# Where the matmul streams and the weights' low halves start in SBUF: the starting bytes modulo 512 of xs, y, z and `lo`

## The chip, the core and the metric

The kernel runs on one core of a Trainium2 chip. The metric is the device time of one execution in microseconds, taken as the median of several runs. A profile of one further execution is read beside it; its span goes from the first to the last recorded instruction.

## The reference

Two residual blocks over 256 tokens of width 2048, in float32. Block 0 mixes with a gated causal convolution of width 31 on one half of the channels and with windowed means on the other; block 1 mixes with a gated causal convolution of width 3. After each mixer stands a gated feed-forward of width 5632.

```python
def conv_pool_mixer(x, ...):
    u = rms_norm(x, norm_g) @ w_in
    a = a_val * sigmoid(a_gate)
    a = silu(layer_norm(causal_depthwise_conv(a, conv_w) + conv_b, ln_g, ln_b))
    p = multiscale_pool(b_in, w_pool, pool_scale)
    return concatenate([a, p], axis=-1) @ w_out

def short_conv_mixer(x, ...):
    u = rms_norm(x, norm_g) @ w_in
    return (gate_b * causal_depthwise_conv(gate_c * v, conv_w)) @ w_out

def swiglu(h, w_gate, w_up, w_down):
    return (silu(h @ w_gate) * (h @ w_up)) @ w_down

def reference(...):
    h = x
    for i in range(DEPTH):
        mixer = conv_pool_mixer if i % 2 == 0 else short_conv_mixer
        h = h + mixer(h, ...)
        h = h + swiglu(rms_norm(h, ffn_norm[i]), w_gate[i], w_up[i], w_down[i])
    return rms_norm(h, final_norm)
```

## The kernel before

**The arithmetic.** Features lie on the 128 partitions and the 256 tokens along the free dimension. Every matrix product runs in the type float32r, with both operands split in two: a weight block of 128 x 128 becomes a rounded high half `hi` (a cast on ScalarE, line 124) and the remainder `lo` (a subtraction on VectorE, line 131; for some pieces of the first mixer on GpSimd). An activation chunk becomes 256 columns of high half followed by 256 columns of remainder, 512 columns or 2048 bytes per partition in one tile (`xs`, `y`, `z` or `cat`). Three of the four products are kept. In a *wide* product (lines 173 and 174) `hi` meets all 512 columns and then `lo` meets the first 256. In a *narrow* one (lines 176 to 178) there are three steps of 256 columns: `hi` with the first half, `hi` with the second, `lo` with the first.

**The weights.** All weights stand in HBM as one row of blocks in the order of use. `fetch` (line 110) brings them in units of up to 16 blocks by DMAs that SyncE issues; `prepare` (line 116) turns pieces of 8 blocks into one `hi` and one `lo` tile each, up to four pieces ahead of use (six buffers of each); `next_block` (line 134) hands them to `product` (line 171). TensorE loads the weights of a step by an instruction of its own, recorded beside the matmul of the step before.

**The stages.** They run one after the other, each a long chain of products with nothing of TensorE's work between:

- first mixer, narrow, 656 blocks: projection from `xs`, pooling and output products from `cat` and `xs`;
- first feed-forward, wide, in two halves of the hidden width. Each half has 22 hidden chunks with two products of 16 blocks from `xs` (704 pairs) and then 16 output chunks of 22 blocks from `y` (352 pairs): 1056 pairs;
- second mixer, wide: 16 chunks of three products from `xs` (768 pairs), then 16 output chunks of 16 blocks from `z` (256 pairs): 1024 pairs;
- second feed-forward, like the first; the last output chunk from `y` is narrow (22 blocks).

`Norm` (line 286) fills `xs` chunk by chunk behind the output product of the stage before; `swiglu` (line 555) fills `y`; the loop at line 586 fills `z`.

**Where the tiles start.** `moving(room, at, n)` (line 222) gives a view of a tile from byte `at` of each partition on. The constants of lines 78 to 85 are these `at`. Blocks, chunks and buffers are whole multiples of 512 bytes long, so the starting byte modulo 512 is the same for every chunk of a stream and for every block of all `hi` or `lo` buffers. From the program's placement of the tiles:

| tile | first byte of the tile | `at` | start modulo 512 | past `hi` modulo 512 |
|---|---|---|---|---|
| `hi` (six buffers) | 101952 | 0 | 64 | 0 |
| `lo` (six buffers) | 126528 | 0 | 64 | 0 |
| `xs`, first mixer | 36160 | 32 | 352 | 288 |
| `xs`, later stages | 36160 | 160 | 480 | 416 |
| `y`, both feed-forwards | 159392 | 64 | 224 | 160 |
| `z` | 159392 | 64 | 224 | 160 |
| `cat` | 184928 | 0 | 96 | 32 |

Of the kernel before, what the change touches and what calls it, by code (L numbers as in the profile page):

```python
# [12 lines left out]
F32R = mybir.dt.float32r  # L13
# [4 lines left out]
P = 128  # L18
T = 256
D = 2048  # L20
NC = D // P
# [4 lines left out]
NH = NF // 2  # L26
# [38 lines left out]
UNIT_AT = [sum(UNITS[:u]) for u in range(len(UNITS))]  # L65

PIECE = 8
PIECES = [(u, o, min(PIECE, n - o)) for u, n in enumerate(UNITS) for o in range(0, n, PIECE)]

LOOK = 4  # L70
AHEAD = 1

# [3 lines left out]


XS_M0 = 32
XS_F0 = 160
XS_M1 = 160  # L80
XS_F1 = 160
Y_F0 = 64
Y_F1 = 64
Z_M1 = 64
CAT = 0

POOL_SPLIT = range(96, 24 * NC + 16 + 7 * NC + 8)
# [7 lines left out]
def block_kernel(ctx: ExitStack, tc: tile.TileContext, xT: bass.AP, xtok: bass.AP, vec: bass.AP, wall: bass.AP, out: bass.AP):  # L95
    nc = tc.nc
    const = ctx.enter_context(tc.tile_pool(name="const", bufs=1))
    act = ctx.enter_context(tc.tile_pool(name="act", bufs=1))
    wst = ctx.enter_context(tc.tile_pool(name="wst", bufs=4))
    whl = ctx.enter_context(tc.tile_pool(name="whl", bufs=6))  # L100
# [9 lines left out]
    def fetch(u):  # L110
        if u < len(UNITS) and u not in loaded:
            n, off = UNITS[u], UNIT_AT[u] * P * P
            loaded[u] = w = wst.tile([P, 16 * P], F32, name="w")
            nc.sync.dma_start(w[:, : n * P], wall[off : off + n * P * P].rearrange("(p f) -> p f", p=P))  # L114

    def prepare(i):
        if i >= len(PIECES) or i in ready:
            return
        u, o, n = PIECES[i]
        fetch(u)  # L120
        w = loaded[u][:, o * P : (o + n) * P]
        hi = whl.tile([P, PIECE * P], F32R, name="hi")
        lo = whl.tile([P, PIECE * P], F32R, name="lo")
        nc.scalar.copy(hi[:, : n * P], w)  # L124
        engine = nc.vector
        if UNIT_AT[u] + o in POOL_SPLIT:
            if relief:
                relief.pop()
            else:
                engine = nc.gpsimd  # L130
        engine.tensor_tensor(out=lo[:, : n * P], in0=w, in1=hi[:, : n * P], op=ALU.subtract)  # L131
        ready[i] = (hi, lo)

    def next_block():
        b, i = cursor
        at = UNIT_AT[PIECES[i][0]] + PIECES[i][1]
        if b == at + PIECES[i][2]:
            ready.pop(i)
            i, at = i + 1, b
        for j in range(i, i + LOOK + 1):  # L140
            prepare(j)
        if i + LOOK < len(PIECES):
            for u in range(PIECES[i + LOOK][0] + 1, PIECES[i + LOOK][0] + AHEAD + 1):
                fetch(u)
        cursor[:] = [b + 1, i]
        hi, lo = ready[i]
        o = (b - at) * P
        return hi[:, o : o + P], lo[:, o : o + P]
# [16 lines left out]
    def drain():  # L165
        while any(queues.values()):
            for q in queues.values():
                if q:
                    q.popleft()[1]()
# [10 lines left out]
    def matmul_chunks(xs, ks, n=1, wide=False, behind=None):  # L180


        accs = [ps.tile([P, 2 * T], F32, name="acc") for _ in range(n)]
        for i, k in enumerate(ks):
            first, last = i == 0, i == len(ks) - 1
            for acc in accs:
                hi, lo = next_block()
                product(acc, hi, lo, xs[:, k, :], first, last, wide)
                tick()
            if behind is not None:  # L190
                behind(k)
        return accs
# [10 lines left out]
    def split(dst, src, scale=None):  # L203

        if scale is None:
            nc.scalar.copy(dst[:, :T], src)
            nc.vector.tensor_tensor(out=dst[:, T:], in0=src, in1=dst[:, :T], op=ALU.subtract)
        else:
            nc.scalar.activation(dst[:, :T], src, AF.Copy, scale=scale)
            nc.vector.scalar_tensor_tensor(out=dst[:, T:], in0=src, scalar=scale, in1=dst[:, :T], op0=ALU.mult, op1=ALU.subtract)  # L210
# [6 lines left out]

    identity = v[:, VECS["identity"] :]
    h = act.tile([P, NC, T], F32, name="h")
    xs_room = act.tile([P, NC * 2 * T + 64], F32R, name="xs")  # L220

    def moving(room, at, n):

        return room[:, at // 4 : at // 4 + n * 2 * T].rearrange("p (c t) -> p c t", c=n)
# [99 lines left out]
    def project(src, ks, norm=None, wide=False, narrow_end=False):  # L324

        for n in range(NC):
            if narrow_end and n == NC - 1:
                wide = False
            (acc,) = matmul_chunks(src, ks, wide=wide)
            if wide:  # L330
                t = phase[0].tile([P, T], F32, name="cross", bufs=3)
                nc.scalar.copy(t, acc[:, T:])
                nc.vector.tensor_tensor(out=h[:, n, :], in0=h[:, n, :], in1=t, op=ALU.add)
            nc.vector.tensor_tensor(out=h[:, n, :], in0=acc[:, :T], in1=h[:, n, :], op=ALU.add)  # L334
            if norm is not None:
                norm.add(n)

    def scaled(acc, r, name, wide=False):
        if not wide:
            s = (phase[0] if name == "pv" else tmp).tile([P, T], F32, name=name, bufs=2)  # L340
            nc.vector.tensor_tensor(out=s, in0=acc[:, :T], in1=r, op=ALU.mult)
            return s
        s = summed(acc, name)
        nc.vector.tensor_tensor(out=s, in0=s, in1=r, op=ALU.mult)
        return s
# [3 lines left out]
    xs = norm.xs  # L349
# [20 lines left out]
    rowsq = const.tile([P, 2], F32, name="rowsq")  # L370
    load(0, 1)
    prepare(0)
    prepare(1)
    load(1, 1)
    prepare(2)
# [8 lines left out]
    with tc.tile_pool(name="m0", bufs=1) as m0, tc.tile_pool(name="ps_side", bufs=2, space=PSUM) as ps_side:  # L384
# [166 lines left out]
        drain()  # L551
        norm = Norm("ffn_norm0", XS_F0)
        project(cat, range(NA), norm)

    def swiglu(norm, following, at):
        with tc.tile_pool(name="ffn", bufs=1) as fp:
            phase[0] = fp
            y = moving(fp.tile([P, NH * 2 * T + 32], F32R, name="y"), at, NH)
            r = None
            for half in range(2):  # L560
                for f in range(NH):
                    (acc_g,) = matmul_chunks(norm.xs, every, wide=True)
                    (acc_u,) = matmul_chunks(norm.xs, every, wide=True)
                    if r is None:
                        r = norm.rstd()
                    gate = scaled(acc_g, r, "gate", True)
                    up = scaled(acc_u, r, "val", True)
                    nc.scalar.activation(gate, gate, AF.Silu)
                    nc.vector.tensor_tensor(out=up, in0=up, in1=gate, op=ALU.mult)
                    split(y[:, f, :], up)  # L570
                project(y, range(NH), following if half else None, wide=True, narrow_end=half and following.final)
# [3 lines left out]

    after = Norm("mix_norm_o", XS_M1)
    swiglu(norm, after, Y_F0)


    norm = Norm("ffn_norm1", XS_F1)  # L580
    with tc.tile_pool(name="m1", bufs=1) as m1:
        phase[0] = m1
        z = moving(m1.tile([P, NC * 2 * T + 32], F32R, name="z"), Z_M1, NC)
        pad = SW - 1
        r = None
        for c in range(NC):
            (acc_c,) = matmul_chunks(after.xs, every, wide=True)
            (acc_v,) = matmul_chunks(after.xs, every, wide=True)
            if r is None:
                r = after.rstd()  # L590
            cg = scaled(acc_c, r, "gate", True)
            vv = scaled(acc_v, r, "val", True)
            cv = m1.tile([P, pad + T], F32, name="cv", bufs=2)
            nc.gpsimd.memset(cv[:, :pad], 0.0)
            nc.vector.tensor_tensor(out=cv[:, pad:], in0=cg, in1=vv, op=ALU.mult)
            wc = VECS["conv_w_o"] + c * SW
            co = m1.tile([P, T], F32, name="co", bufs=2)
            nc.vector.tensor_scalar(out=co, in0=cv[:, :T], scalar1=v[:, wc : wc + 1], scalar2=None, op0=ALU.mult)
            for k in range(1, SW):
                nc.vector.scalar_tensor_tensor(out=co, in0=cv[:, k : k + T], scalar=v[:, wc + k : wc + k + 1], in1=co, op0=ALU.mult, op1=ALU.add)  # L600
            (acc_b,) = matmul_chunks(after.xs, every, wide=True)
            bg = scaled(acc_b, r, "pv", True)
            nc.vector.tensor_tensor(out=bg, in0=bg, in1=co, op=ALU.mult)
            split(z[:, c, :], bg)
        project(z, every, norm, wide=True)


    last = Norm("final_norm", final=True)
    swiglu(norm, last, Y_F1)
    halves = rsqrt_of(*last.sums, scale=1.0 / D, halves=True)  # L610
    with tc.tile_pool(name="fin", bufs=1) as fin:
# [91 lines left out]
```

## Time and profile before

| | us |
|---|---|
| median of 3 runs | 2094.08 (2093.9 to 2096.47) |
| the profiled execution | 2094.95 |
| its span | 2093.2 |
| TensorE busy in the span (matmuls) | 2070.2 |
| weight loads, beside them | 1850.5 |
| VectorE busy | 1383.1 |
| ScalarE busy | 1061.8 |
| first wide pair of the first feed-forward starts at | 256.5 |
| first wide pair of the second mixer starts at | 990.1 |
| first wide pair of the second feed-forward starts at | 1346.4 |

In the profile PE is TensorE's matmuls, PEld its weight loads (which run beside the matmuls), DVE is VectorE, ACT ScalarE, POOL GpSimd and SP SyncE. `L173` is line 173 of the kernel. Matmuls are pipelined: a recorded duration reaches beyond the start of the next matmul, so the rate of a stream is read from starts, and not from durations. Busy time counts the union of the intervals.

### The profile page before, as it was taken

Reading aid. Unit: us, or ns where it says so; the run is one execution under the profiler, and the core shown is the slowest. Engines: PE = TensorE matmul, PEld = TensorE weight load, DVE = VectorE, ACT = ScalarE, POOL = GpSimd, SP = SyncE. Lnnn points to the kernel's source line nnn. Section 1 sums busy time; section 2 is a strip of 40 time slices with the busy share of each in tenths; the row PEclk is TensorE's granted clock in tenths of the full one; section 3 lists DMA queues with packets and bytes.
Section 4 is the critical chain, followed back from the end, with each engine's and each line's share of the span. In section 5 each row is a group of like instructions: output and inputs, shape, how many; then the busy total and the mean of one; then the engine's idle time right before and its main releaser. Section 6 shows DMA issues by size and latency. Waiting matters only on the chain.

```text
span 2093.2 us, 31608 instructions
## 1 busy us (share of the span) xinstructions
PE 2070.2 (99%) x12584; PEld 1850.5 (88%) x12584; DVE 1383.1 (66%) x1979; ACT 1061.8 (51%) x1571; POOL 200.5 (10%) x180
## 2 busy tenths in 40 slices
PE   8998999999999999999999999999999999999998
PEld 8998988888888888888888888888888888888887
DVE  6998766666556666666777777766666556666654
ACT  7886654444444444455444445554444444444453
POOL 2995200000000000011000001100000000000011
PEclk9999999999999999999999999999999999999999
DMA  8555455555555455555555555455555555555551
GB/s 322 190 199 181 151 190 184 193 189 186 196 184 198 182 195 188 188 195 183 189 191 184 198 182 199 181 186 197 182 195 187 190 193 184 199 183 195 187 191 71
DMA packets 56884, 395.53 MB, mean 189 GB/s; under 512 B 6432, under 2 KB 7200, under 8 KB 9760
## 3 DMA queue, kind: packets, MB, share of 16 engines
q1 hardware_dynamic: 56736, 393.52, 51.9%
q8 instruction: 98, 1.61, 0.3%
q14 instruction: 50, 0.41, 0.1%
HBM read 391.39 MB, written 2.10 MB: 188 GB/s over the span
## 4 chain that ended last, share of the span: by engine, by line
PE 98%; DMA 1%; DVE 1%; ACT 0%; SPq 0%; issue 0%; DVEq 0%; ACTq 0%
PE acc L173 57%; PE acc L174 29%; PE acc L176 4%; PE acc L178 4%; PE acc L177 3%; DMA rows<-in_xtok 0%; DMA h<-in_xT 0%; DVE res L620 0%; ACT hi L124 0%; PE st L252 0%; DVE lo L131 0%; PE st L283 0%; SPq L114 0%; ACT conv L492 0%; PE idle L258 0%
## 5 line engine op out<-in xcount | busy, mean ns | idle before, releaser
L131 DVE TENSOR_TENSOR lo<-w,hi 128x1024 fp32r<-128x1024 f32 (+1 forms) x691 | 846.2, 1225 | 634.3 <-ACT hi L124 630.1
L124 ACT CAST hi<-w 128x1024 fp32r<-128x1024 f32 (+1 forms) x740 | 775.5, 1049 | 963.9 <-PE acc L173 615.9
L173 PE MATMUL acc<-xs,hi 128*128 128x512 f32 x3584 | 1243.2, 392 | 0.0
L174 PE MATMUL acc<-xs,lo 128*128 128x256 f32 x3584 | 1002.3, 280 | 0.0
L173 PEld LDWEIGHTS acc<-xs,hi 128*128 128x128 f32 x3584 | 672.7, 188 | 148.5
L174 PEld LDWEIGHTS acc<-xs,lo 128*128 128x128 f32 x3584 | 672.7, 188 | 0.1
L173 PE MATMUL acc<-y,hi 128*128 128x512 f32 x1386 | 480.4, 392 | 0.0
L174 PE MATMUL acc<-y,lo 128*128 128x256 f32 x1386 | 386.8, 280 | 0.0
L173 PEld LDWEIGHTS acc<-y,hi 128*128 128x128 f32 x1386 | 259.9, 188 | 57.2
L174 PEld LDWEIGHTS acc<-y,lo 128*128 128x128 f32 x1386 | 260.2, 188 | 0.4
L314 POOL TENSOR_TENSOR sumsq<-sumsq,sq 128x256 f32<-128x256 f32 x56 | 59.0, 1053 | 1593.0 <-ACT sq L312 1593.0
L176 PE MATMUL acc<-xs,hi 128*128 128x256 f32 x512 | 142.7, 282 | 5.2 <-ACT hi L124 4.2
L177 PE MATMUL acc<-xs,hi 128*128 128x256 f32 x512 | 142.2, 280 | 0.0
L178 PE MATMUL acc<-xs,lo 128*128 128x256 f32 x512 | 140.2, 282 | 0.1
L131 POOL TENSOR_TENSOR lo<-w,hi 128x1024 fp32r<-128x1024 f32 x49 | 118.5, 2440 | 41.4 <-ACT hi L124 41.3
L176 PEld LDWEIGHTS acc<-xs,hi 128*128 128x128 f32 x512 | 96.9, 190 | 6.1 <-ACT hi L124 4.8
L177 PEld LDWEIGHTS acc<-xs,hi 128*128 128x128 f32 x512 | 96.9, 189 | 0.0
L178 PEld LDWEIGHTS acc<-xs,lo 128*128 128x128 f32 x512 | 95.4, 190 | 0.5 <-DVE lo L131 0.5
L173 PE MATMUL acc<-z,hi 128*128 128x512 f32 x256 | 88.7, 392 | 0.0
L198 ACT COPY cross<-acc 128x256 f32<-128x256 f32 x224 | 81.4, 363 | 0.0
L174 PE MATMUL acc<-z,lo 128*128 128x256 f32 x256 | 71.4, 280 | 0.0
L334 DVE TENSOR_TENSOR h<-acc,h 128x256 f32<-128x256 f32 x112 | 47.2, 423 | 18.3 <-PE acc L178 11.9
(134 smaller groups left out, 1199.3 us busy)
## 6 DMA issues: line engine op xcount, KB each, us to landing
w<-in_wall SPq DMA_DIRECT2D x365, 1024.0 KB, 4.8
w<-in_wall SPq DMA_DIRECT2D x7, 512.0 KB, 7.3
rows<-in_xtok SPq DMA_DIRECT2D x2, 1024.0 KB, 8.1
h<-in_xT SPq DMA_DIRECT2D x7, 256.0 KB, 7.2
out<-res SPq DMA_DIRECT2D x2, 512.0 KB, 2.8
out<-res SPq DMA_DIRECT2D x2, 384.0 KB, 2.8
v<-in_vec SPq DMA_DIRECT2D x1, 260.0 KB, 6.6
h<-in_xT SPq DMA_DIRECT2D x2, 128.0 KB, 2.3
```

The costliest lines, as they stand in the source:

```text
L124: nc.scalar.copy(hi[:, : n * P], w)
L131: engine.tensor_tensor(out=lo[:, : n * P], in0=w, in1=hi[:, : n * P], op=ALU.subtract)
L173: nc.tensor.matmul(acc, hi, x, start=first, stop=False, skip_group_check=True)
L174: nc.tensor.matmul(acc[:, T:], lo, x[:, :T], start=False, stop=last, skip_group_check=True)
L176: nc.tensor.matmul(acc[:, :T], hi, x[:, :T], start=first, stop=False)
L177: nc.tensor.matmul(acc[:, :T], hi, x[:, T:], start=False, stop=False)
L178: nc.tensor.matmul(acc[:, :T], lo, x[:, :T], start=False, stop=last)
L198: nc.scalar.copy(t, acc[:, T:])
L314: nc.gpsimd.tensor_tensor(out=self.sums[0], in0=self.sums[0], in1=sq, op=ALU.add)
L334: nc.vector.tensor_tensor(out=h[:, n, :], in0=acc[:, :T], in1=h[:, n, :], op=ALU.add)
```

## The change

`lo` and the stream tiles get 128 spare float32 columns each (`lo` had none, `xs` 64, `y` and `z` 32). `prepare` puts the low halves at an offset `at` into their tile that depends on the part of the weight row (`LO_AT`, keyed by the first block of the part). Some `at` constants differ, and `y` has one for each half of a feed-forward.

```diff
+_m0, _ffn = 24 * NC + 16 + NC * NC, 3 * NH * NC
+LO_AT = {0: 0, _m0: 0, _m0 + _ffn: 320, _m0 + 2 * _ffn: 0, _m0 + 2 * _ffn + 64 * NC: 448, _m0 + 3 * _ffn + 64 * NC: 416}
+
...
 XS_M0 = 32
-XS_F0 = 160
-XS_M1 = 160
+XS_F0 = 32
+XS_M1 = 224
 XS_F1 = 160
-Y_F0 = 64
-Y_F1 = 64
-Z_M1 = 64
+Y_F0 = (448, 448)
+Y_F1 = (64, 64)
+Z_M1 = 128
 CAT = 0
...
         hi = whl.tile([P, PIECE * P], F32R, name="hi")
-        lo = whl.tile([P, PIECE * P], F32R, name="lo")
+        lo = whl.tile([P, PIECE * P + 128], F32R, name="lo")
+        at = LO_AT[max(b for b in LO_AT if b <= UNIT_AT[u] + o)] // 4
+        lo = lo[:, at : at + PIECE * P]
...
-    xs_room = act.tile([P, NC * 2 * T + 64], F32R, name="xs")
+    xs_room = act.tile([P, NC * 2 * T + 128], F32R, name="xs")
...
-            y = moving(fp.tile([P, NH * 2 * T + 32], F32R, name="y"), at, NH)
+            y_room = fp.tile([P, NH * 2 * T + 128], F32R, name="y")
             r = None
             for half in range(2):
+                y = moving(y_room, at[half], NH)
...
-        z = moving(m1.tile([P, NC * 2 * T + 32], F32R, name="z"), Z_M1, NC)
+        z = moving(m1.tile([P, NC * 2 * T + 128], F32R, name="z"), Z_M1, NC)
```

The longer tiles move what is placed behind them: the `hi` buffers start 256 bytes later (320 modulo 512), the `lo` tiles at 320 modulo 512 too, before their own offset; `y`, `z` and the tiles of the first mixer start 3328 bytes later. With the new `at` the distances modulo 512 are these:

| part | blocks | stream past `hi`, before | after | stream past `lo`, before | after |
|---|---|---|---|---|---|
| first mixer, `xs` / `cat` | 656 | 288 / 32 | 32 / 32 | 288 / 32 | 32 / 32 |
| first feed-forward, half 0, `xs` / `y` | 1056 | 416 / 160 | 32 / 32 | 416 / 160 | 32 / 32 |
| first feed-forward, half 1 | 1056 | 416 / 160 | 32 / 32 | 416 / 160 | 224 / 224 |
| second mixer, `xs` / `z` | 1024 | 416 / 160 | 224 / 224 | 416 / 160 | 224 / 224 |
| second feed-forward, half 0, `xs` / `y` | 1056 | 416 / 160 | 160 / 160 | 416 / 160 | 224 / 224 |
| second feed-forward, half 1 | 1056 | 416 / 160 | 160 / 160 | 416 / 160 | 256 / 256 |

## The prediction

> **What bounds the kernel now.** First the page: the span, the share of each engine, the granted clock, the chain that ended last and the costliest groups.
>
> ```profile
> span 2093.2 us, 31608 instructions
> PE 2070.2 (99%) x12584; PEld 1850.5 (88%) x12584; DVE 1383.1 (66%) x1979; ACT 1061.8 (51%) x1571; POOL 200.5 (10%) x180
> ...
> PEclk9999999999999999999999999999999999999999
> ...
> PE 98%; DMA 1%; DVE 1%; ACT 0%; SPq 0%; issue 0%; DVEq 0%; ACTq 0%
> ...
> L131 DVE TENSOR_TENSOR lo<-w,hi 128x1024 fp32r<-128x1024 f32 (+1 forms) x691 | 846.2, 1225 | 634.3 <-ACT hi L124 630.1
> L124 ACT CAST hi<-w 128x1024 fp32r<-128x1024 f32 (+1 forms) x740 | 775.5, 1049 | 963.9 <-PE acc L173 615.9
> L173 PE MATMUL acc<-xs,hi 128*128 128x512 f32 x3584 | 1243.2, 392 | 0.0
> L174 PE MATMUL acc<-xs,lo 128*128 128x256 f32 x3584 | 1002.3, 280 | 0.0
> ...
> L173 PE MATMUL acc<-y,hi 128*128 128x512 f32 x1386 | 480.4, 392 | 0.0
> ...
> L173 PE MATMUL acc<-z,hi 128*128 128x512 f32 x256 | 88.7, 392 | 0.0
> ```
>
> TensorE is the bound: 98% of the chain is its own work, and before L173 and L174 it never sat idle (0.0). The other engines wait for it: ScalarE's cast of the weights (L124) spent 615.9 us waiting for matmuls to free a buffer. There are 3584 + 1386 + 256 = 5226 wide pairs (L173 and L174), each 512 columns against a high half and then 256 against its low half. What a wide pair takes from start to start is therefore what decides.
>
> Next the windows, one stretch inside each of three stages (length, then busy time and count of PE, PEld, DVE, ACT and POOL, then clock and DMA).
>
> ```profile
> 623.70:867.80 244.10, 244.10 (x1410) 214.86 (x1409) 157.21 (x218) 117.83 (x175) 0.00 (x0) 1.00 0.53 190
> 867.80:989.80 122.00, 122.00 (x706) 107.37 (x705) 79.80 (x93) 62.43 (x91) 14.05 (x14) 1.00 0.53 190
> 1257.40:1346.10 88.70, 88.70 (x514) 78.06 (x513) 65.05 (x84) 48.98 (x79) 13.55 (x14) 1.00 0.53 190
> ```
>
> TensorE is busy for the whole of every stretch at granted clock 1.00, VectorE for 73% at most (65.05 of 88.70), ScalarE for 55%, DMA for 53%. No cover is short.
>
> Then the tile views of the streams, each cut to one stage, give the rate (duration min/median/max, first and last start): xs and y of the first feed-forward, z of the short convolution.
>
> ```profile
> L173 PE MATMUL acc<-xs,hi x704: 391/392/392, 624.0 to 867.7; 128*128 128x512 f32 x176
> ```
> ```profile
> L173 PE MATMUL acc<-y,hi x301: 391/392/392, 519.6 to 623.6; 128*128 128x512 f32 x151
> ```
> ```profile
> L173 PE MATMUL acc<-z,hi x220: 391/392/392, 1269.8 to 1345.7; 128*128 128x512 f32 x110
> ```
>
> 243.7 / 703, 104.0 / 300 and 75.9 / 219 us are all 346.6 to 346.7 ns per pair, though xs starts 416 bytes past the high halves modulo 512 and y and z 160. The timeline divides a pair:
>
> ```profile
> 800.06 0.39 PE L173 MATMUL acc<-xs,hi 128*128 128x512 f32 x1
> 800.07 0.19 PEld L174 LDWEIGHTS acc<-xs,lo 128*128 128x128 f32 x1
> 800.29 0.28 PE L174 MATMUL acc<-xs,lo 128*128 128x256 f32 x1
> 800.29 0.19 PEld L173 LDWEIGHTS acc<-xs,hi 128*128 128x128 f32 x1
> 800.41 0.39 PE L173 MATMUL acc<-xs,hi 128*128 128x512 f32 x1
> ```
>
> About 0.23 us for 512 columns and 0.12 for 256. The low half is loaded while the stream passes the high half, and the next high half while it passes the low one. So two distances count, stream to low half in the long step and stream to high half in the short one, and the change sets just these two.
>
> **The change part by part.** (1) *Instructions.* None is added, removed or reordered; no wait or DMA is new. xs, y and z are longer tiles, and VectorE writes `lo` at another byte of a longer tile: its 1225 ns have no reason to change. A piece of 8 weight blocks lasts TensorE 8 x 346.7 = 2.77 us; the cast and the subtraction need 1.05 and 1.23 us on two engines. That cover hides this edit; only a subtraction of over twice its length would show. Value 0.
>
> (2) *The first mixer.* Its narrow steps (three of 256 columns per block) have xs at 288 past the halves now and at 32 afterwards; `cat` is at 32 before and after. The rates now:
>
> ```profile
> L176 PE MATMUL acc<-xs,hi x229: 277/280/281, 59.9 to 139.7; 128*128 128x256 f32 x115
> ```
> ```profile
> 226.05 0.28 PE L176 MATMUL acc<-cat,hi 128*128 128x256 f32 x1
> ...
> 256.15 0.28 PE L176 MATMUL acc<-cat,hi 128*128 128x256 f32 x1
> ```
> ```profile
> L176 PE MATMUL acc<-y,hi x22: 277/280/282, 2072.3 to 2079.7; 128*128 128x256 f32 x22
> ```
> ```profile
> 2072.30 0.28 PE L176 MATMUL acc<-y,hi 128*128 128x256 f32 x1
> ...
> 2079.69 0.28 PE L176 MATMUL acc<-y,hi 128*128 128x256 f32 x1
> ```
>
> xs at 288: 79.8 / 228 = 350.0 ns per block. `cat` at 32: 30.10 us hold 86 blocks, 350.0 ns. They agree, so this move costs 0; with the gap found in (3) as bound on both sides, 656 blocks are within 1.2 us. The third pair is the narrow last chunk, y at 160: 22 starts, 7.39 / 21 = 351.9 ns.
>
> (3) *The wide parts.* After the change stream past high half / stream past low half are 32/32 (first feed-forward, half 0), 32/224 (half 1), 224/224 (second mixer), 160/224 and 160/256 (second feed-forward); before it both were 416 for xs and 160 for y and z. Of these new settings the trace shows none in wide steps. Bounds from the nearest rows:
>
> - *That a distance counts at all*: 351.9 against 350.0 ns, the same 768 columns per block at 160 and at 32. 1.9 ns.
> - *The dear end*: the whole of one y stage, its first pairs included.
>
> ```profile
> L173 PE MATMUL acc<-y,hi x352: 391/392/400, 501.9 to 623.6; 128*128 128x512 f32 x176
> L174 PEld LDWEIGHTS acc<-y,lo x352: 187/188/194, 501.9 to 623.6; 128*128 128x128 f32 x176
> ```
>
> Right after a stage starts a 512-column step took up to 400 ns where 392 is the rule, and a low half's load 194 where 188 is: both longer in the same stage, as when load and stream hold each other up. 8 ns on every pair would be 5226 x 8 = 42 us.
> - *The cheap end*: loads with next to no stream beside them, four to a row, at the second mixer's norm.
>
> ```profile
> 1001.03 0.53 PEld L252 LDWEIGHTS st<-ones,sumsq 128*128 128x128 f32 x4
> 1001.48 0.53 PEld L252 LDWEIGHTS st<-ones,sq 128*128 128x128 f32 x4
> 1001.93 0.19 PEld L173 LDWEIGHTS acc<-xs,hi 128*128 128x128 f32 x1
> ```
>
> Eight loads in 0.90 us: 112.5 ns each. From the duration rows a long step is 112 ns over a short one (392 - 280), so 512 columns at that rate alone are 224 ns. 224 + 112.5 = 336.5 ns would be a pair without any loss: 10.2 ns under 346.7, 53 us in all, an estimate for the extreme. The Trainium skill, "TensorE: Matmul & The Clock Gate", section "Back-to-back issue gap", gives N / 2.4 + 2.5 ns a step, an estimate of 325 ns a pair; by it the extreme would be 113 us. No run here shows that rate.
>
> I take 1.9 ns per pair, lost: the nearest row in kind (settled, the same columns, only the distance different), and lost because every odd duration around 392 and 188 lies above the rule by far more than below (400 and 194 against 391 and 187): phases other than the settled one have cost time here. Against it, the 1.9 ns themselves say that 32 is the better place for short steps; I come to that as a rival. 5226 x 1.9 = 9.9 us.
>
> *Sum*: 2093.2 + 0 + 0 + 9.9 = 2103.1 us of span. The profiled execution took 2094.95 us, 1.75 over its span, so 2104.9; the median, 2094.08, is 0.9 below that execution. **2104 us.**
>
> **The rivals.** "Same" is within 0.2%, some 4.2 us, about what a measurement of this kernel can tell from no change.
>
> *A, the forecast: off the settled distances a pair loses a little.* 2104; its own range runs from just over 2098 (0.9 ns) to 2117 (4.4 ns, about half the dear end). For: the 1.9 ns gap and the lengthened first pairs. Against: 416 and 160 agree to 0.1 ns.
>
> *B, faster: the low halves' loads stop disturbing the long step.* The place is line 173 where the stream is 224 past the low half: 1056 + 1024 + 1056 = 3136 pairs. A long step takes some 229.4 ns (346.7 less 117.3, a third of the 351.9) and could fall to 224: 5.4 x 3136 = 16.9 us, 2077. If the short step of all pairs fell as well by the 0.6 ns between 351.9 / 3 and 350.0 / 3, 3.3 us more: 2074. It decides once the three parts gain over 4.2 us / 3136 = 1.3 ns a pair and the others lose nothing. For: 32 beats 160 in narrow steps, and 10 ns a pair are unexplained. Against: nothing shows that 224 is a free place.
>
> *C, no change: the rate doesn't depend on distances.* Stream and load would be read side by side, and 346.7 be the pair's own length: 2094. For: 416 equals 160, 288 equals 32. Against: the 351.9, and the 400 with the 194. The Trainium skill says this outright: "SBUF — State Buffer", section "Who interferes with whom", gives TensorE two independent read ports, one for the moving operand and one for the weights, and has it never wait on anyone; by that rule the time stays. The trace agrees in the equal rates and disagrees in the 1.9 ns. That the change misses the distances it names would end here too; the tiles' starting bytes give those it names.
>
> *D, much slower: the two reads meet all along.* The 8 ns of the first pairs become the rule in all five parts: 2094 + 42 = 2136. It needs the self-settling seen after each start to fail.
>
> **How the numbers follow.** A 0.42, B 0.27, C 0.20, D 0.11. Faster 0.27, same 0.20, slower 0.42 + 0.11 = 0.53. The range goes from B with its short steps and 1.2 us of the first mixer, 2074 - 1 = 2073, to D with that on top, 2137. What is left out, about 0.15, lies toward the cheap end and above D. A's own range is 2098.5 to 2117.
>
> **What would show it.** TensorE must stay busy throughout in every stage with the same 12584 matmuls; otherwise part (1) was wrong. The first mixer must still show 350.0 ns per block. The tile views cut by stage give the five new rates beside 346.7: A wants some 348.6 in most parts, B 341 in the three parts with 224 and nothing lost elsewhere, C 346.7 everywhere, D 354 and long weight loads. The starts of lines 173 and 174 tell which of the two distances it was: a long step that changes names the low half, a short one the high half. If the five parts differ with both signs, one price for all was wrong, and the sum is that of five separate ones.

## The result, and the profile after

| | before | after | ratio (95% interval) |
|---|---|---|---|
| median, us | 2094.08 | 2109.49 | 1.0067 (1.0053 to 1.0081) |
| span of the profiled execution, us | 2093.2 | 2106.7 | |

The change makes the kernel 0.7% slower: 13.5 us of span. The page of the changed kernel, the lines that answer to those of before (lines 173 and 174 are now 178 and 179, line 131 is 136):

```profile
span 2106.7 us, 31608 instructions
PE 2085.0 (99%) x12584; PEld 1857.1 (88%) x12584; DVE 1383.7 (66%) x1979; ACT 1061.2 (50%) x1571; POOL 200.4 (10%) x180
...
PE 98%; DMA 1%; DVE 1%; ACT 0%; SPq 0%; issue 0%; DVEq 0%; ACTq 0%
...
L136 DVE TENSOR_TENSOR lo<-w,hi 128x1024 fp32r<-128x1024 f32 (+1 forms) x691 | 846.6, 1226 | 646.2 <-ACT hi L129 641.8
...
L178 PE MATMUL acc<-xs,hi 128*128 128x512 f32 x3584 | 1253.3, 394 | 0.0
L179 PE MATMUL acc<-xs,lo 128*128 128x256 f32 x3584 | 1006.2, 281 | 0.0
```

As many matmuls, as much work on the other engines, the subtraction at 1226 ns where it took 1225, and TensorE still never idle ahead of a wide step. The time is in TensorE's own rate. Its busy time grew by 14.8 us (2085.0 - 2070.2), its idle time fell by 1.3.

The tile views, cut to a settled stretch of one stage each, divide it (duration min/median/max, first and last start): the first feed-forward's half 1, xs and then y; the second mixer's xs; the second feed-forward's half 0, xs and y; its half 1, xs and y.

```profile
L178 PE MATMUL acc<-xs,hi x703: 389/393/397, 623.9 to 868.8; 128*128 128x512 f32 x176
```
```profile
L178 PE MATMUL acc<-y,hi x307: 396/396/396, 884.9 to 993.0; 128*128 128x512 f32 x154
```
```profile
L178 PE MATMUL acc<-xs,hi x709: 392/402/402, 1014.6 to 1264.8; 128*128 128x512 f32 x178
```
```profile
L178 PE MATMUL acc<-xs,hi x612: 391/397/400, 1389.8 to 1604.9; 128*128 128x512 f32 x153
```
```profile
L178 PE MATMUL acc<-y,hi x305: 389/389/389, 1621.6 to 1726.0; 128*128 128x512 f32 x153
```
```profile
L178 PE MATMUL acc<-xs,hi x703: 393/393/393, 1726.7 to 1970.1; 128*128 128x512 f32 x176
```
```profile
L178 PE MATMUL acc<-y,hi x297: 392/394/394, 1981.9 to 2085.5; 128*128 128x512 f32 x149
```

Divide last minus first start by one less than the count: 244.9 / 702 = 348.9 ns a pair, 108.1 / 306 = 353.3, 250.2 / 708 = 353.4, 215.1 / 611 = 352.0, 104.4 / 304 = 343.4, 243.4 / 702 = 346.7, 103.6 / 296 = 350.0. Before, all of these were 346.7. Even the recorded duration of a long step shows it (389 to 402; it was 392).

| part | past high / past low | xs, ns a pair | y or z, ns a pair | change of the stages, us |
|---|---|---|---|---|
| first feed-forward, half 0 | 32/32 | 346.7 | 346.7 | 0 |
| half 1 | 32/224 | 348.9 | 353.3 | +1.6 +2.2 |
| second mixer | 224/224 | 353.3 | 353.3 | +4.9 +1.7 |
| second feed-forward, half 0 | 160/224 | 352.0 | **343.3** | +3.6 -0.9 |
| half 1 | 160/256 | 346.7 | 350.0 | 0 +1.0 |

A stage's change is the difference of its length from first to last start; the rates are those of its settled stretch, and the first 26 pairs of each y stage and of z still run at the rate of the xs before them. The sum is +14.1 us. The first wide pair starts at 256.1 us, where it was 256.5; in the kernels below, which have the same distances in the first mixer, it starts anywhere from 255.2 to 257.1, so these 0.4 us can't be put down to the change.

The odd thing is that xs and y of one part have the *same* two distances and yet different rates, and that one of them is quicker than anything before. The chain of waits of the changed kernel, where y of the second feed-forward's half 0 begins (start, length, engine and line):

```profile
1604.35 0.23 PE acc L178
...
1613.86 0.23 PE acc L178
1614.09 0.12 PE acc L179
1614.21 0.47 PE acc L178 x2
1614.68 0.24 PE acc L179 x2
1614.92 0.23 PE acc L178
```

From 1604.35 to 1613.86 lie 27 pairs of 352 ns, the last of xs and then y: y *starts* at the rate of xs. At 1614.21 two long steps and then two short ones stand side by side (`x2`). The kernel's text gives no such order; the compiled program has it once in the second output chunk of each wide output projection, before and after the change, at the step from the 26th pair to the 27th. Below it is called a *break*. A few pairs behind it the pairs take 343.3.

### The profile page after: what moved, and what is told of

It is laid out like the page before. It is cut to its first block, busy times and chain, and to the rows that moved or that the text cites. A ratio compares the mean times of both kernels' runs of the same rounds, so it can differ in the third digit from the quotient of the medians.

```text
span 2106.7 us, 31608 instructions
## 1 busy us (share of the span) xinstructions
PE 2085.0 (99%) x12584; PEld 1857.1 (88%) x12584; DVE 1383.7 (66%) x1979; ACT 1061.2 (50%) x1571; POOL 200.4 (10%) x180
## 4 chain that ended last, share of the span: by engine, by line
PE 98%; DMA 1%; DVE 1%; ACT 0%; SPq 0%; issue 0%; DVEq 0%; ACTq 0%
PE acc L178 57%; PE acc L179 29%; PE acc L181 4%; PE acc L183 3%; PE acc L182 3%; DMA rows<-in_xtok 0%; DMA h<-in_xT 0%; DVE res L626 0%; ACT hi L129 0%; PE st L257 0%; DVE lo L136 0%; PE st L288 0%; SPq L117 0%; ACT conv L497 0%; PE idle L263 0%; ACT rows L371 0%
## 5 line engine op out<-in xcount | busy, mean ns | idle before, releaser
L136 DVE TENSOR_TENSOR lo<-w,hi 128x1024 fp32r<-128x1024 f32 (+1 forms) x691 | 846.6, 1226 | 646.2 <-ACT hi L129 641.8
```

## The experiments

The first theory after the result, **rhythms**: the two distances set which rates a stream of pairs can settle in (a rhythm is one such settled rate), there may be more than one, and a break in the order of steps moves it from one to the other. Its rivals: the rate belongs to the tile's own place (xs and y lie at different addresses); one of the two distances alone decides; what counts is where VectorE writes, not where TensorE reads. Six of the ten kernels below ran once; for these the argument rests on the rates within the trace, which for one setting and rhythm agree between kernels to a few tenths of a ns, as read from the rounded starts.

### Only the streams moved

```diff
-LO_AT = {0: 0, _m0: 0, _m0 + _ffn: 320, _m0 + 2 * _ffn: 0, _m0 + 2 * _ffn + 64 * NC: 448, _m0 + 3 * _ffn + 64 * NC: 416}
+LO_AT = {0: 0, _m0: 0, _m0 + _ffn: 0, _m0 + 2 * _ffn: 0, _m0 + 2 * _ffn + 64 * NC: 0, _m0 + 3 * _ffn + 64 * NC: 0}
```

> Only the stream half of the change: streams at 32, 224 and 160 past the high halves, every low half at the high ones' place (both distances equal in every part). The two distances act together (theory): 32/32 and 160/160 stay at 346.7 ns a pair, 224/224 keeps its 353.3, so the first feed-forward's half 1 and the second feed-forward fall back to the rates of before and only the second mixer's 4.9 + 1.7 us remain: span about 2093.2 + 6.6 = 2099.8 us. Rival (the streams' place alone is what costs, the low halves' place is idle): the rates stay those of the changed kernel, 2106.7 us.

Span 2099.8 us, as expected; that it fits to the tenth is chance, since the five runs had spans of 2098.6 to 2101.9. The median of 2102.21 is 1.0035 (1.0021 to 1.0049) times that of before. 32/32 and 160/160 run at 346.7, 224/224 at 353.3. The places of the streams alone, with both distances equal, cost the second mixer's 6.6 us; the rest of the loss came with the low halves' places.

### 160/224 in all wide parts

```diff
-LO_AT = {0: 0, _m0: 0, _m0 + _ffn: 320, _m0 + 2 * _ffn: 0, _m0 + 2 * _ffn + 64 * NC: 448, _m0 + 3 * _ffn + 64 * NC: 416}
+LO_AT = {0: 0, _m0: 448, _m0 + _ffn: 448, _m0 + 2 * _ffn: 448, _m0 + 2 * _ffn + 64 * NC: 448, _m0 + 3 * _ffn + 64 * NC: 448}
...
-XS_F0 = 32
-XS_M1 = 224
+XS_F0 = 160
+XS_M1 = 160
...
-Y_F0 = (448, 448)
+Y_F0 = (64, 64)
...
-Z_M1 = 128
+Z_M1 = 64
```

> Streams 160 past the high halves and 224 past the low ones in all five wide parts. In the changed kernel this setting ran at 352.0 ns in xs and at 343.3 ns in y after the one place where two long steps stand side by side. Theory of rhythms (the same addresses have several settled rates, and a break in the order of steps chooses): xs 352.0 and y and z 343.3 again in every part, 3584 x 5.3 - 1642 x 3.3 = +13.6, span about 2107 us; if xs takes the quick rhythm in some parts, less, down to 2076 us. Rival (xs and y differ by their own places in SBUF, whatever the order): the same 352.0 and 343.3, but y at 343.3 from its first pair on.

Span 2101.9, median 2103.18 (ratio 1.0039, 1.0026 to 1.0052). The expectation that y and z always take the quick rate was wrong, and that is what taught most. The tile views of the first feed-forward, in order of time: xs and y of half 0, xs and y of half 1.

```profile
L178 PE MATMUL acc<-xs,hi x583: 391/397/400, 300.0 to 504.8; 128*128 128x512 f32 x195
```
```profile
L178 PE MATMUL acc<-y,hi x325: 389/389/398, 514.7 to 625.9; 128*128 128x512 f32 x163
```
```profile
L178 PE MATMUL acc<-xs,hi x703: 389/389/389, 626.6 to 867.6; 128*128 128x512 f32 x176
```
```profile
L178 PE MATMUL acc<-y,hi x288: 391/397/400, 889.9 to 991.0; 128*128 128x512 f32 x144
```

351.9, 343.2, 343.3 and 352.3 ns. xs takes both rates in this kernel, and y takes both: the rate doesn't belong to the tile. From half 0's y to half 1's xs nothing breaks the order and the quick rate is handed on, across a change of tile; at the break in half 1's y it is lost. So a break doesn't lead to the quick rhythm; in these cases it leads to the other one.

It doesn't always. In the second mixer of the same kernel z has its break too, and keeps 352.0 ns on both sides:

```profile
1271.95 0.63 PE L178 MATMUL acc<-z,hi 128*128 128x512 f32 x2
```
```profile
L178 PE MATMUL acc<-z,hi x209: 391/397/400, 1279.7 to 1352.9; 128*128 128x512 f32 x105
```

The 25 pairs ahead of 1271.95 take 352.0 ns, and behind it 73.2 / 208 = 351.9. The order of the break is that of y; what differs in the trace is where it falls. The 352.0 ns are a cycle of five pairs of about 344, 352, 353, 353 and 358 ns. The breaks of y that led to 343.3 fall behind the second 353, that of z behind the first. Whether this point in the cycle is the reason was not tested.

The norm's own small products, which interrupt the head of an xs stage twice, act on the rhythm as well. In all three xs stages behind a norm of this kernel xs runs at 343.3 ns between the two interruptions and at 352.0 behind the second, whether it began at 343.3 (first feed-forward) or at 352.0 (the two later ones). That is how xs behind a norm comes to 352.0 here.

### A break in the middle of each xs stage

```diff
+SWAP = (11,)
...
+                if swap is not None and i in (swap, swap + 1):
+                    x = xs[:, k, :]
+                    nc.tensor.matmul(acc, hi, x, start=first, stop=False, skip_group_check=True)
+                    if i == swap:
+                        held = lo, x
+                    else:
+                        for b, m in (held, (lo, x)):
+                            nc.tensor.matmul(acc[:, T:], b, m[:, :T], start=False, stop=False, skip_group_check=True)
+                else:
+                    product(acc, hi, lo, xs[:, k, :], first, last, wide)
...
-                    (acc_g,) = matmul_chunks(norm.xs, every, wide=True)
+                    (acc_g,) = matmul_chunks(norm.xs, every, wide=True, swap=2 if f in SWAP else None)
...
+            (acc_c,) = matmul_chunks(after.xs, every, wide=True, swap=2 if c in SWAP else None)
```

> The changed kernel, with two blocks of one chunk in the middle of each xs stage (chunk 11) taken as long, long, short, short steps, as y has it near its start; the same work and addresses. Theory of rhythms: from chunk 11 on xs takes the rate that y has after its own such place: 348.9 to 353.3 ns in the first feed-forward's half 1, 352.0 to 343.3 in the second one's half 0, 346.7 to 350.0 in its half 1, no change in half 0 of the first (346.7) and in the second mixer (353.3). Rival (a rate belongs to the tile's addresses alone): no rate changes at chunk 11.

The chain of waits at the inserted break in half 0 of the second feed-forward (the two blocks of the break are lines 196 and 201 in this kernel), and the tile views of xs ahead of it and behind it:

```profile
1481.91 0.23 PE acc L179
1482.15 0.12 PE acc L180
1482.26 0.23 PE acc L179
1482.50 0.12 PE acc L180
1482.62 0.23 PE acc L179
1482.85 0.12 PE acc L180
1482.97 0.47 PE acc L196 x2
1483.44 0.24 PE acc L201 x2
```
```profile
L179 PE MATMUL acc<-xs,hi x257: 391/397/400, 1389.9 to 1480.0; 128*128 128x512 f32 x129
```
```profile
L179 PE MATMUL acc<-xs,hi x328: 389/389/389, 1489.7 to 1602.0; 128*128 128x512 f32 x164
```

90.1 / 256 = 352.0 ns ahead, 112.3 / 327 = 343.4 behind; same tile, same weights' places, same work. In the first feed-forward's half 1 the same break takes 348.9 to 353.3, in the second one's half 1 346.7 to 350.0, and 32/32 and 224/224 stay. All five as expected. And the y of the second feed-forward's half 0, at 343.3 in the changed kernel, runs at 352.0 here: it enters at 343.3 and its own break throws it back. That the tile's place decides is refuted. But not every pair of distances goes both ways: y of the first feed-forward's half 1 enters its break at 353.3 and stays there, and y of the second one's half 1 enters at 350.0 and stays.

### Modulo 256 or 512

```diff
-LO_AT = {0: 0, _m0: 0, _m0 + _ffn: 320, _m0 + 2 * _ffn: 0, _m0 + 2 * _ffn + 64 * NC: 448, _m0 + 3 * _ffn + 64 * NC: 416}
+LO_AT = {0: 0, _m0: 448, _m0 + _ffn: 192, _m0 + 2 * _ffn: 448, _m0 + 2 * _ffn + 64 * NC: 448, _m0 + 3 * _ffn + 64 * NC: 192}
...
-XS_F0 = 32
-XS_M1 = 224
+XS_F0 = 416
+XS_M1 = 160
...
-Y_F0 = (448, 448)
+Y_F0 = (320, 320)
...
-Z_M1 = 128
+Z_M1 = 64
```

> Distances that agree modulo 256 in four parts: stream past high / past low half 416/480 and 416/224 in the first feed-forward, 160/224 in the second mixer and in half 0 of the second feed-forward, 160/480 in its half 1. If the distances count modulo 256, all five show the rates of 160/224: 352.0 or 343.3 ns and no others. If they count modulo 512, the parts with 416 or 480 show rates of their own, such as 346.7 or 350.0.

Only 352.0 and 343.3, in the same order as in the kernel with 160/224 throughout; its span is 2102.9, the other one's 2101.9. 416/480, 416/224 and 160/480 are the same as 160/224: the distances count modulo 256. That is also why 416 and 160 agreed before. A modulus of 128 doesn't do: 32/224 and 160/224 differ by 128 in one distance and have different rates.

### Everything 96 bytes further on

```diff
+    shift = const.tile([P, 24], F32, name="shift")
+    nc.gpsimd.memset(shift, 0.0)
```

> The changed kernel with high halves, low halves and all streams 96 bytes further on: every distance is the same, every place modulo 256 another. If the rate is set by the distances between what TensorE's two reads take, each part keeps its rate (346.7; 348.9 and 353.3; 353.3; 352.0 and 343.3; 346.7 and 350.0), span 2106.7. Rival (the places themselves count, or what another engine writes at fixed places): the rates of the parts change.

Every stage keeps its rate, and the changes of rate fall at the same breaks (353.3 ns in y of the first feed-forward's half 1, 343.4 in y of the second one's half 0, and so on); span 2105.9. The distances count; a move of all places together by 96 bytes does nothing.

### The high half taken twice

```diff
-            nc.tensor.matmul(acc[:, T:], lo, x[:, :T], start=False, stop=last, skip_group_check=True)
+            nc.tensor.matmul(acc[:, T:], hi, x[:, :T], start=False, stop=last, skip_group_check=True)
```

> The changed kernel with the short wide step taking the high half once more in place of the low one (the low halves' products are left out); the low halves are made and written where they were. If it is the place that TensorE loads from that counts, both distances are now the stream's distance from the high half, and the rates are those of the streams alone: 346.7 in both feed-forwards, 353.3 in the second mixer, span about 2099.8 us. Rival (what counts is where VectorE writes the low halves beside the stream): the rates of the changed kernel stay, 348.9 and 353.3, 352.0 and 343.3, 350.0, span 2106.7 us.

Span 2100.0 us. The tile views of xs in the first feed-forward's half 1 and of z:

```profile
L178 PE MATMUL acc<-xs,hi x704: 390/390/390, 624.2 to 867.9; 128*128 128x512 f32 x176
```
```profile
L178 PE MATMUL acc<-z,hi x236: 392/397/402, 1269.8 to 1352.9; 128*128 128x512 f32 x118
```

243.7 / 703 = 346.7 and 83.1 / 235 = 353.6 ns, and 346.7 in both halves of the second feed-forward. VectorE still writes the low halves where the changed kernel has them; the rates have gone over to those of the place that TensorE loads from. The compiled program has no break here, so the evidence is two xs stages, which have no break in the changed kernel either: 348.9 to 346.7 ns in the first feed-forward's half 1, and 352.0 to 346.7 in the second one's half 0.

### Other distances

Two kernels with five new settings each and the break at chunk 11.

> New pairs of distances, with a break at chunk 11 of each xs stage to see a second rhythm: stream past high / past low half 160/192 and 160/128, 192/224, 128/224 and 128/192. The theory gives settled rates between 343.3 and 353.3 ns as so far, in steps of 3.33 ns or a simple fraction of it. If the low half's distance alone decided, 192/224 and 128/224 would show 343.3 or 352.0. A rate under 343.3 would say that the quick rhythm of 160/224 still holds waits.

> The same for 0/224 and 0/64, 96/224, 64/224 and 64/128. As for the survey before it: rates from 343.3 to 353.3 ns by the theory, 343.3 or 352.0 in the parts with 224 if the low half's distance alone decided, under 343.3 if waits are left in the quick rhythm.

| past high / past low | ns a pair (two values: ahead of and behind a break) |
|---|---|
| 160/192 | 353.3 |
| 160/128 | 350.7 |
| 192/224 | 351.1 |
| 128/224 | about 351.4 |
| 128/192 | 346.7 |
| 0/224, 0/64 | 346.7 |
| 96/224 | 350.0 and 346.7 in xs, 346.7 and 350.0 in z |
| 64/224, 64/128 | 346.7 |

Spans 2113.1 and 2095.8. None is under 346.7, only 96/224 shows a second rate, and 224 past the low half goes with anything from 343.3 to 353.3, so the low half's distance alone doesn't decide. In 0/64 the steps shift against each other without a gain: 113.3 ns for the short step (117.5 at 160/160) and 233.4 for the long one (229.2).

### The quick rhythm held

160/224 throughout, and the swap of the third experiment at chunk 2 of the xs stages that follow a norm, and once per output projection beside the break that is there, so that the two together undo each other.

```diff
+                    (acc_g,) = matmul_chunks(norm.xs, every, wide=True, swap=2 if f in SWAP and not half else None)
...
-            (acc,) = matmul_chunks(src, ks, wide=wide)
+            (acc,) = matmul_chunks(src, ks, wide=wide, swap=8 if wide and n == 1 else None)
```

> 160 past the high halves and 224 past the low ones in all wide parts, with breaks of order (two blocks taken long, long, short, short) added in the first half's xs stages behind the norm (chunk 2) and once in each output projection of the wide stages beside the break that is there already. If a break changes the rhythm over, from 352.0 to 343.3 ns and back: xs at 343.3 after chunk 2, y and z back at 343.3 behind the second break; 5226 x 3.3 = 17.4 us less than before, and some 192 pairs ahead of the breaks at 8.7 more: 2093.2 - 17.4 + 1.7 = 2077.5 us span. Rival (a break leads to a rhythm that the place chooses, not to the other one): y and z stay at 352.0, 1642 x 8.7 = 14.3 more, about 2092 us.

Span 2077.1 us, 0.4 from what was expected (the four runs had 2076.8 to 2080.4). The median is 2079.64, 0.9932 (0.9915 to 0.9949) times that of before: quicker than both kernels, with the same steps in an order that differs in a few places. Its page, and the tile views of a stretch of xs and of y in the first half:

```profile
PE 2055.8 (99%) x12584; PEld 1845.8 (89%) x12584; DVE 1383.2 (67%) x1979; ACT 1060.6 (51%) x1571; POOL 200.5 (10%) x180
```
```profile
L179 PE MATMUL acc<-xs,hi x627: 389/389/390, 284.7 to 499.6; 128*128 128x512 f32 x157
```
```profile
L179 PE MATMUL acc<-y,hi x307: 389/389/390, 514.8 to 619.9; 128*128 128x512 f32 x154
```

214.9 / 626 = 343.3 and 105.1 / 306 = 343.5 ns. The breaks at chunk 2 fall behind the 344 of the five-pair cycle, another point than the breaks before, and lead to 343.3 too. The control has the same breaks at 160/160, the distances of before:

> The breaks of the kernel that ran in 2079.6 us, at the same steps, but with all low halves at the high ones' place and all streams at 160, the distances of before. If the breaks only choose among the rhythms that a pair of distances has, and 160/160 has one, all wide parts stay at 346.7 ns and the time is that of before, 2094 us. Rival (the breaks themselves gain): about 2080 us.

2095.04 us, 1.0002 (0.9993 to 1.0012) times before, and 346.7 ns in every wide part. The breaks by themselves do nothing; they matter where the distances allow more than one rhythm.

## Why the prediction was right, and where it wasn't

**The bound, and parts (1) and (2)** held. TensorE stayed busy throughout, the subtraction kept its time, and the first mixer its rate: xs at 32 has 350.0 ns a block, where it had 350.0 at 288.

**Part (3), direction and size.** Forecast was +9.9 us of span, 13.5 came; 2104 us against 2109.49, inside A's own range. The reason given, that leaving the settled distances costs some nanoseconds a pair in TensorE's own steps, is what the runs show. But the term was one price for all pairs, 1.9 ns, and that price is not what the stages paid. It came from narrow steps, as the gap between 160 and 32; in wide steps just this move, to 32/32 in the first feed-forward's half 0, costs 0. The ten stages have prices from -3.3 to +6.7 ns, and three of them cost nothing. The prediction's last section names this case ("If the five parts differ with both signs, one price for all was wrong"), and stage by stage it is what happened, though no whole part came out quicker. That the sum came near is luck: 14.1 us over 5226 pairs is 2.7 ns on average, made of stages that have nothing to do with the gap it was taken from.

**The argument for the sign was weak, and it rested on a misreading.** It took the 400 ns of long steps and the 194 ns of loads in a y stage for the first pairs after a start, and as a sign that every other phase costs time. The same stage before the change, cut at the break:

```profile
L173 PE MATMUL acc<-y,hi x25: 391/391/392, 501.9 to 510.2; 128*128 128x512 f32 x25
```
```profile
L173 PE MATMUL acc<-y,hi x26: 391/392/400, 510.6 to 519.3; 128*128 128x512 f32 x26
```

The first 25 pairs are settled; the 400 stands behind the break, whose two long steps start at 510.58 and 510.81, and the load of 194 does too. So nothing settled after a start of y, and the rows showed the way through a break back into the one rhythm of 160/160, not how good the rhythm at other distances is. 160/224 behind a break is another phase, and 3.3 ns quicker.

**Which of the two steps changed** was to tell which distance it was. With the stream 160 past the high halves throughout, moving the low half from 160 to 224 takes the long step from 229.2 ns to 234.0 in one rhythm and 226.7 in the other, and the short step from 117.5 to 118.0 and 116.7. Most of the change is in the long step, beside which the low half is loaded. The distance to the high half counts too: with 224 past the low half, the rates differ with 32, 160 and 224 past the high one.

**Rival B** named the place (line 173, stream 224 past the low half) and had half of the mechanism: at 160/224 there is a rate below 346.7, at 343.3 and not at B's 341, with 2.5 of the 3.3 ns gained in the long step. But 224 as such is no free place (32/224 and 224/224 are slower), and which rate is taken was outside all the rivals: none had a stream with two settled rates at one address.

**Rival C** is refuted for the five parts together, though two kinds of distance do share one rate: 32/32 is 346.7 like 160/160. The rule that the prediction set beside it, in the Trainium skill, "SBUF — State Buffer", section "Who interferes with whom" (two independent read ports, and TensorE waits on no one), doesn't hold here as far as speed goes: with only the two reads moved against each other, a pair settles anywhere from 343.3 to 353.3 ns. **Rival D** needed 8 ns on every pair; the worst stage lost 6.7.

**The cheap end**, 336.5 ns, was not reached by any of the settings tried. Its two parts were nearly met, each in another setting: a short step of 113.3 ns at 0/64 (the lone load took 112.5) and a long one of 226.7 at 160/224 (the estimate was 224).

What stays open: by what means the place of one read against the other costs time, why a break of order moves a stream to another rhythm, and why some breaks don't. The runs show that the place of the load against the stream decides, modulo 256, which rates there are, and they show at which steps the rate changes; they don't show how.

## What to carry to other kernels

Where TensorE is never idle and its steps are still longer than their columns explain, compare the rate of start to start by stage, and look at where the moving operand stands against the weights modulo 256; it was worth -1% to +2% of a pair here. Then look at whether the rate changes inside a stage with nothing else changing: a stream can have two settled rates, and one reordered pair of steps can move it from one to the other, though not at every place. Judge a placement by the settled rates of all its stages and not by one stage or by the total, since a setting with a quicker rhythm (160/224) came out 0.4% slower until its rhythm was held.

## What the runs showed of the hardware that was not expected

- The settled rates are multiples of 3.33 ns or averages of them over a few pairs: 343.3, 346.7, 350.0 and 353.3 ns are 103 to 106 such units; 348.9 is three pairs in 314, 352.0 five pairs in 528.
- One setting can have two settled rates (160/224: 352.0 and 343.3; 32/224: 348.9 and 353.3; 160/256: 346.7 and 350.0; 96/224: 350.0 and 346.7). They last until the next break or other interruption, through whole stages, and are handed on from one tile to the next. A swap of two steps changed from one to the other in both directions at 160/224 and 96/224, and in one direction only at 32/224 (353.3 stayed) and 160/256 (350.0 stayed). At 160/224 breaks met at 343.3 led to 352.0; of those met at 352.0 most led to 343.3 and two, both in z, changed nothing. 32/32, 160/160 and 224/224 showed only one rate.
- Distances that differ by 256 bytes behave alike in every case tried.
